# Hybrid linear-attention and window-attention block: longer planned distances, fewer places for small steps, two moved loads

## The chip, the cores and the metric

The kernel runs on one core of one Trainium2 chip. The metric is the device time of one execution in microseconds, the median of several runs. The engines are TensorE (PE, with its weight loads PEld), VectorE (DVE), ScalarE (ACT), GpSimd (POOL) and SyncE (SP), which issues nearly all DMAs.

## The reference, cut to what matters

The input is 2048 tokens of 1024 values in float32. Branch A is a gated delta rule with four heads of 128 (in the kernel in blocks of 128 tokens). Branch B is attention over a window of 128 tokens with eight query heads, two key heads and a sink logit per head.

```python
h = x @ w_in                          # q, k, v, z, b, a of A; q, k, v, z of B; two gates
dq, dk, dv = split(silu(causal_short_conv(h[:, :1536], conv_w)))
# branch A, per head, state S (128 x 128):
#   S <- exp(g_t) S;  S <- S + k_t (beta_t (v_t - S^T k_t))^T;  o_t = S^T q_t
#   evaluated in blocks with the inverse of (1 + lower triangle of beta k k^T decay)
y_a = rmsnorm(o_a) * dn_norm_w * silu(z_a)
# branch B
p   = softmax(q k^T / 8 in the band, with the sink in the denominator)
y_b = (p v) * silu(z_b)
merged = sigmoid(gate_a) * (y_a @ w_branch[0]) + sigmoid(gate_b) * (y_b @ w_branch[1])
r = ALPHA * x + merged @ w_out
y = (r - mean(r)) * rsqrt(var(r) + eps) * ln_g + ln_b
```

## The kernel before, in words

The 2048 tokens are worked in four chunks of 512. Every dense product is made from three matmuls, because each operand is split into a high and a low part: L184 (high by high), L185 and L186 (high by low), all into the PSUM tiles `mm`. The weights are split once, in the first chunk, and kept in DRAM (`kw_...`); in chunks two to four SP loads them back into `wb`, which has four buffers (L160; L158 for the last output weights). A load waits on SP's queue until its buffer is free, and what stands behind it on the queue waits too.

A chunk is a list of pieces: the string `ORDER` (kv, k0, q0, ... are projections, `g` a gate, `p` a part of the output projection of the chunk before, `w0` and `w1` the queries of branch B, `z` the gates of branch A's output), then eight `branch_b`, the first pieces of the next chunk, and eight `branch_a`. After `p` number 3 the norm of the chunk before starts (`layer_norm`).

Between dense matmuls stand small steps, which are chains over several engines. Of branch A: `front` (K^T L382, R L395, KK L406, q^T L426, KQ L432), an inverse on DVE (L947, L948) that goes through DRAM (`scrm`, `scrp`), `levels` (lv1 to lv4: L470, L477, L486, L491), and `back`. `back` is one chain through the four blocks: kS (L517, reads the state S) -> bt (DVE, L519) -> NEW (L522, L525) -> wc (DVE, L524) -> UPD (L528, L530) -> S (DVE, L529) -> the next block's kS. Of branch B: qT (L584, after the rope on DVE, L893 to L899) and per block ATT (scores, L610, L611) -> softmax (DVE L618 to L628, ACT L623 to L630) -> pT (two lots of four transposes, L637, each copied by ACT, L639) -> psY (L645) -> DVE and ACT write `yBh`, `yBl` (L650 to L653). These two tiles are in the same buffers as the rows that `layer_norm` works on, and attention starts when the norm is done. The norm is 32 times one L727 and one L728 on DVE; its table (gain and bias) comes in four quarters, `s<-in_lnp`, by SP.

PE's order is fixed in the program by the class `Order`, a planner with a clock of its own, `now`. Every dense piece advances `now` by a planned cost and then calls `run()`, which puts in every small step whose time has come. After a step its task is due again a fixed distance later: LAT_B within front and levels, LAT_S within back, LAT_SM from ATT to pT, LAT_D before lv1, LAT_Q from rope to qT, and so on. These distances are plan numbers; on the chip a step that comes too early waits. Where the program needs a task finished (`finish`), the planner jumps its clock without dense work, so that the task's steps stand one behind the other. The orders on DVE, ACT, POOL and SP follow from the same program, and each engine works its queue in order.

Of the kernel before, what the change touches and what calls it, by code (L numbers as in the profile page):

```python
# [16 lines left out]
P = 128  # L17
D = 1024
# [20 lines left out]

LAT_INV, LAT_B, LAT_S, LAT_N, LAT_SM, LAT_D, LAT_M, LAT_K, LAT_Q, LAT_Y, LAT_F, LAT_W = 29600, 2700, 2300, 7700, 9200, 11000, 9000, 1400, 7900, 11500, 4100, 2300  # L40
FIRST = ("h01", "h00", "h02")


ORDER_FIRST = "start g kv w0 g k1 g g q1 g g g z0 v1 g z1 k2 q2 v2 w1 k3 g q3 g v3 g g g g z2 z3 g g"
ORDER = "kv k0 q0 v0 k1 p p p p q1 g w0 v1 z0 k2 q2 v2 g g g k3 z1 g q3 g w1 v3 g g g g z2 g g g z3 g g g"

# [17 lines left out]
def build(tc, xt, xn, wk, wg, par, lnp, cst, out, seq=2048):  # L64
    nc = tc.nc
    NCH = seq // T
    with ExitStack() as ctx:
# [169 lines left out]
        def start(c):  # L237
# [25 lines left out]
            st.spawn("front0", front(c, 0), LAT_F)  # L263

        def window_kv(c):

            ww, more = [], ([w.rearrange("p (k c) -> p k c", k=2) for w in split(("kv", i), wk[i // 2, :, 528 * (i % 2):528 * (i % 2) + 528], 528)]
                            for i in range(4))
            ba = sm.tile([P, NB, 8], F32, name="ba")
            c.vs = [c.prev.vs[4] if c.i else None]  # L270
            for b0 in (0, 2):
                pss = [mm.tile([P, T], F32, name="mm")[:, :264] for _ in range(2)]
                yield from prod_tc(pss, (b0, b0 + 1), c.xh, c.xl, ww if b0 else kept(more, ww), lambda k: load_x(c, k))
                for b, ps in zip((b0, b0 + 1), pss):
# [9 lines left out]
            st.spawn("decay", decays(c, ba), LAT_Y)  # L284

# [13 lines left out]
        def decays(c, ba):  # L299
            c.beta, c.g = gates_small(nc, sm, ba, nea, prm[:, P_DTB:P_DTB + 4])  # L300
            flat = lambda a: a.rearrange("p b h -> p (b h)")
            new = lambda name: sm.tile([P, NB, NH], F32, name=name)
            c.nG, c.kd, c.neG, c.eGl = new("nG"), new("kd"), new("neG"), new("eGl")
            psg = pd.tile([P, T], F32, name="pd")
            tri = sm.tile([P, P], F32, name="wc", bufs=1)
            nc.vector.tensor_scalar(tri, dmask, 0.0, None, ALU.is_ge)
            nc.tensor.matmul(psg[:, :16], tri, flat(c.g), start=True, stop=True)
            nc.tensor.matmul(psg[:, 16:32], ones, flat(c.g), start=True, stop=True)
            G = psg[:, :16].rearrange("p (b h) -> p b h", h=NH)
            gg = sm.tile([P, NB, 2, NH], F32R, name="ghl", bufs=1)  # L310
# [8 lines left out]
            yield 2 * 426, 2000  # L319
# [49 lines left out]
        def front(c, h):  # L369
# [21 lines left out]
            nc.vector.tensor_scalar(nci, cc, -1.0, None, ALU.mult)  # L391
            yield 4 * PE_T, LAT_B

# [8 lines left out]
            nc.vector.tensor_tensor(qd, qd, q4, ALU.mult)  # L402
            yield PE_R, LAT_B
            psKK = p4()
# [5 lines left out]
            t0 = st.now  # L410
            yield 4 * PE_F, LAT_B

# [14 lines left out]
            for b in range(NB):  # L427
                nc.scalar.activation(junk, psQ[:, b], AF.Square, accum_out=qsum[:, b:b + 1])
            yield 4 * PE_T, LAT_B
            psKQ = p4()  # L430
# [4 lines left out]
            q_ = t4("q_", 2)  # L435
            st.spawn(f"levels{h}", levels(c, h, m2, q_), max(LAT_B, t0 + LAT_INV - st.now))
            st.spawn(f"back{h}", back(c, h, k4, q_, ktl, qd, dt, cc, ksum, qsum), max(LAT_B, t0 + LAT_INV - st.now))
            yield 4 * PE_F, 0

        def inverse(h, su, xi):  # L440

            with tc.issue_after(next(i for i in reversed(nc.cur_bb.bb.instructions) if i.engine == mybir.EngineType.DVE)):
                nc.vector.memset(view(su, 33, [[66, 16]]), 0.0)
# [4 lines left out]
        def levels(c, h, m2, q_):  # L448
# [11 lines left out]
            yield 0, LAT_D  # L460
            for i in range(4):
# [9 lines left out]
            for s in range(2):  # L471
                copy[s](x_[hi[s], :, :32], ps[s][hi[s], :, :32])
            yield 8 * PE_Q, LAT_B
            ps = [p4(), pp.tile([P, NB, P], F32, name="pp")]
# [13 lines left out]
            yield 4 * PE_T, LAT_B  # L488
# [4 lines left out]
            yield 4 * PE_T, LAT_B  # L493

        def back(c, h, k4, q_, ktl, qd, dt, cc, ksum, qsum):
# [16 lines left out]
            st.done.add(f"vdone{h}")  # L512
            yield 4 * PE_T, LAT_B
            psO = p4()
            for b in range(NB):
# [9 lines left out]
                nc.tensor.matmul(psO[:, b], qd[:, b], S[:, h], start=True, stop=False)  # L525
                yield 2 * PE_F, LAT_S
# [4 lines left out]
                yield 2 * PE_F, LAT_S  # L531

# [28 lines left out]
        def window_q(c, gp):  # L561
# [6 lines left out]
            for b0 in (0, 2):  # L568
# [25 lines left out]
        def attend(c, gp):  # L594
# [8 lines left out]
            for b in range(NB):  # L603
# [108 lines left out]
        def layer_norm(c):  # L712
            fs = []
            for b in range(NB):
# [118 lines left out]
class Order:  # L833
# [190 lines left out]
```

## Time and profile before

| what | value |
|---|---|
| time, median of 3 runs | 1668.41 us (1666.62 to 1669.23) |
| the profiled execution's own time | 1672.24 us |
| its span | 1670.40 us |
| PE busy | 1618.9 us, 97% of the span |
| PE's share of the chain that ended last | 82% |
| DVE, ACT, POOL busy | 969.3, 596.2, 92.9 us |
| mean granted TensorE clock | 0.986 of full |

The profiled execution has 1.84 us outside its span and took 3.83 us more than the median. PE is busy nearly all the time, and its matmuls are pipelined, so that a busy PE is read by the distance of the starts. A wait of PE is in brackets in the timeline, with the instruction that released it. A granted clock of 1.00 in a stretch is the 2.4 GHz level, 0.50 the 1.2 GHz level.

### The profile page before, as it was taken

How to read it: one execution, taken by the hardware profiler on the slowest of the kernel's cores; microseconds unless marked ns; L12 is line 12 of the kernel's file. 1: busy time of each engine (PE TensorE's matmuls, PEld its weight loads, DVE VectorE, ACT ScalarE, POOL GpSimd, SP SyncE). 2: the span in 40 equal slices, each digit the busy share in tenths (PEclk: the TensorE clock that was granted, in tenths of full speed). 3: DMA queues.
4: the chain of work that ended last, by engine and by line, in shares of the span. 5: the costliest groups of instructions: out<-in, count | busy, mean ns of one | idle time of the engine just before them, and what ended most of it. 6: DMA issues, size and time to landing. Idle time of an engine off the chain costs nothing.

```text
span 1670.4 us, 26939 instructions
## 1 busy us (share of the span) xinstructions
PE 1618.9 (97%) x9846; PEld 1368.2 (82%) x9846; DVE 969.3 (58%) x3005; ACT 596.2 (36%) x1688; POOL 92.9 (6%) x142
## 2 busy tenths in 40 slices
PE   8999999999998999999999999999999999999998
PEld 6877878787987878788898878888889887878788
DVE  5777687459566656323747774623482866462145
ACT  3565455424213533441301452433230254233110
POOL 2100000000000001000000000000000100000000
PEclk9999999999999999999999999999999999999999
DMA  8876575776867446457666644646666654555862
GB/s 310 260 232 222 184 245 190 244 235 216 273 207 213 135 130 168 142 163 237 191 213 205 199 128 145 172 137 190 202 190 210 221 162 119 166 162 145 284 214 83
DMA packets 189157, 323.37 MB, mean 194 GB/s; under 512 B 31072, under 2 KB 45408, under 8 KB 188896
## 3 DMA queue, kind: packets, MB, share of 16 engines
q1 hardware_dynamic: 185184, 316.40, 60.6%
q0 software_dynamic: 3840, 5.25, 1.5%
q8 instruction: 78, 1.28, 0.3%
q14 instruction: 55, 0.45, 0.1%
HBM read 244.97 MB, written 71.37 MB: 189 GB/s over the span
## 4 chain that ended last, share of the span: by engine, by line
PE 82%; DVE 7%; DMA 7%; ACT 2%; issue 1%; SPq 1%; POOL 0%; DVEq 0%; ACTq 0%; POOLq 0%
PE mm L184 22%; PE mm L186 22%; PE mm L185 22%; PE pp L645 2%; PE pp L637 2%; DMA s<-in_lnp 2%; DMA w<-in_xt 1%; PE pp L610 1%; PE pp L611 1%; PE pd L432 1%; DVE wb L165 1%; PE pd L517 1%; PE pd L528 1%; DMA xl<-kw_o 1%; PE pd L406 1%
## 5 line engine op out<-in xcount | busy, mean ns | idle before, releaser
L184 PE MATMUL mm<-xh,wb 128*128 128x512 f32 x1128 | 468.6, 415 | 0.0
L186 PE MATMUL mm<-xh,wb 128*128 128x512 f32 x1128 | 448.0, 397 | 0.0
L185 PE MATMUL mm<-xl,wb 128*128 128x512 f32 x1128 | 446.8, 396 | 0.0
L186 PEld LDWEIGHTS mm<-xh,wb 128*128 128x128 f32 x1128 | 213.7, 189 | 50.3
L184 PEld LDWEIGHTS mm<-xh,wb 128*128 128x128 f32 x1128 | 214.5, 190 | 45.6 <-issue 6.5
L185 PEld LDWEIGHTS mm<-xl,wb 128*128 128x128 f32 x1128 | 215.2, 191 | 38.8
L184 PE MATMUL mm<-wb,xh 128*128 128x256 f32 (+1 forms) x384 | 113.5, 296 | 1.8 <-DVE kr L899 0.9
L184 PE MATMUL mm<-wb,s 128*128 128x256 f32 x384 | 110.4, 287 | 0.0
L185 PE MATMUL mm<-wb,xh 128*128 128x256 f32 (+1 forms) x384 | 108.9, 284 | 0.0
L186 PE MATMUL mm<-wb,xl 128*128 128x256 f32 (+1 forms) x384 | 108.7, 283 | 0.0
L185 PE MATMUL mm<-wb,s 128*128 128x256 f32 x384 | 108.4, 282 | 0.0
L186 PE MATMUL mm<-wb,s 128*128 128x256 f32 x384 | 108.4, 282 | 0.0
L165 DVE TENSOR_TENSOR wb<-w,wb 128x512 fp32r<-128x512 f32 (+1 forms) x110 | 75.4, 686 | 46.3 <-ACT wb L164 45.5
L164 ACT ACTIVATE wb<-w 128x512 fp32r<-128x512 f32 (+1 forms) x110 | 69.1, 629 | 84.4 <-PE mm L186 58.1
L623 ACT ACTIVATE s<-s,nm 128x256 f32<-128x256 f32 (+1 forms) x128 | 62.5, 490 | 57.1 <-DVE nm L620 56.6
L947 DVE TENSOR_TENSOR xt<-su,xi 128x16 f32<-128x16 f32 (+15 forms) x256 | 76.3, 298 | 5.3
L948 DVE TENSOR_REDUCE xi<-xt 128x8 f32<-128x16 f32 (+15 forms) x256 | 74.6, 291 | 4.9
L184 PEld LDWEIGHTS mm<-wb,xh 128*128 128x128 f32 x384 | 72.9, 190 | 2.7 <-issue 2.5
L184 PEld LDWEIGHTS mm<-wb,s 128*128 128x128 f32 x384 | 73.1, 190 | 0.8
L185 PEld LDWEIGHTS mm<-wb,xh 128*128 128x128 f32 x384 | 72.9, 190 | 0.5
L185 PEld LDWEIGHTS mm<-wb,s 128*128 128x128 f32 x384 | 73.0, 190 | 0.1
L186 PEld LDWEIGHTS mm<-wb,s 128*128 128x128 f32 x384 | 73.0, 190 | 0.0
(660 smaller groups left out, 2997.4 us busy)
## 6 DMA issues: line engine op xcount, KB each, us to landing
wb<-kw_h SPq DMA_DIRECT2D x96, 512.0 KB, 4.1
wb<-kw_g SPq DMA_DIRECT2D x96, 512.0 KB, 4.0
w<-in_wg SPq DMA_DIRECT2D x106, 256.0 KB, 4.2
wb<-kw_b SPq DMA_DIRECT2D x48, 512.0 KB, 4.4
wb<-kw_o SPq DMA_DIRECT2D x36, 512.0 KB, 4.1
kw_h<-wb SPq DMA_DIRECT2D x32, 512.0 KB, 3.9
kw_g<-wb SPq DMA_DIRECT2D x32, 512.0 KB, 3.7
wb<-kw_q SPq DMA_DIRECT2D x24, 512.0 KB, 3.9
```

Of the source, the lines that this page charges most:

```text
L164: nc.scalar.activation(hi, raw, AF.Copy)
L165: nc.vector.tensor_tensor(lo, raw, hi.bitcast(F32), ALU.subtract)
L184: nc.tensor.matmul(ps, sh, mh, start=(first and i == 0), stop=False, skip_group_check=shared)
L185: nc.tensor.matmul(ps, sh, ml, start=False, stop=False, skip_group_check=shared)
L186: nc.tensor.matmul(ps, sl, mh, start=False, stop=(last and i == n), skip_group_check=shared)
L406: nc.tensor.matmul(psKK[:, b], k4[:, b], k4[:, b], start=True, stop=True)
L432: nc.tensor.matmul(psKQ[:, b], k4[:, b], q4[:, b], start=True, stop=True)
L623: nc.scalar.activation(ss[v][:, g, k0:], ss[v][:, g, k0:], AF.Exp, bias=nm[:, v, g:g + 1], scale=0.125, accum_out=su[:, v, g:g + 1])
L637: nc.tensor.transpose(psp[:, kb, g], ss[v][:, g, P * kb:P * kb + P], ident)
L645: nc.tensor.matmul(psY[64 * v:64 * v + 64], c.vs[b + kb][:, 64 * v:64 * v + 64], pTs[v][:, kb], start=(kb == kbs[0]), stop=(kb == 1))
L947: nc.vector.tensor_tensor(tx[:, :, :, :n], u, x, ALU.mult)
L948: nc.vector.tensor_reduce(xi[:, :, i:i + 2], tx[:, :, :, :n], AX.X, ALU.add)
```

## The change

In chunks two to four the distances within front, levels and back are 600 ns longer, ATT to pT 2300, before lv1 2000, rope to qT 2600, and the step in `decays` 1500. In `ORDER` the piece `w1` stands one gate earlier. Each quarter of the norm's table is asked for one quarter ahead, and the norm's planned distances are longer. Each half of the last output weights is issued behind the last SP instruction placed so far. Last, `run()` is called only when 1900 ns of the planner's clock have gone by since the last time.

```diff
+LAT_B, LAT_S, LAT_SM, LAT_D, LAT_Q, LAT_Y, LAT_G = (2700, 3300), (2300, 2900), (9200, 11500), (11000, 13000), (7900, 10500), (11500, 11500), (2000, 3500)
-ORDER = "kv k0 q0 v0 k1 p p p p q1 g w0 v1 z0 k2 q2 v2 g g g k3 z1 g q3 g w1 v3 g g g g z2 g g g z3 g g g"
+ORDER = "kv k0 q0 v0 k1 p p p p q1 g w0 v1 z0 k2 q2 v2 g g g k3 z1 g q3 w1 g v3 g g g g z2 g g g z3 g g g"
+        latest = lambda engine: next(i for i in reversed(nc.cur_bb.bb.instructions) if i.engine == engine)
...
-                yield PE_F, LAT_S
+                yield PE_F, LAT_S[c.i > 0]
...
-                yield 8 * PE_T, LAT_SM
+                yield 8 * PE_T, LAT_SM[c.i > 0]
...
+            def load_lg(eg):
+                lgs.append(pa.tile([P, 2, 256], F32, name="s"))
+                nc.sync.dma_start(out=lgs[eg], in_=bass.AP(tensor=lnp.tensor, offset=lnp.offset + 256 * eg, ap=[[0, P], [D, 2], [1, 256]]))
+            load_lg(0)
...
-                yield None, 2500
+                yield None, 2600
...
-                lg = pa.tile([P, 2, 256], F32, name="s")
-                nc.sync.dma_start(out=lg, in_=bass.AP(tensor=lnp.tensor, offset=lnp.offset + 256 * eg, ap=[[0, P], [D, 2], [1, 256]]))
+                if eg < 3:
+                    load_lg(eg + 1)
+                lg = lgs[eg]
...
-                    yield None, 1800
+                    yield None, 2200
...
+            st.quantum = 1900.0 if i else 0.0
...
                 if i == NCH - 1 and d in (1, 4):
-                    last_weights(c, d // 3)
+                    with tc.issue_after(latest(mybir.EngineType.SP)):
+                        last_weights(c, d // 3)
...
                 self.now += dur
-                self.run()
+                if self.now >= self.next:
+                    self.run()
+                    self.next = self.now + self.quantum
```

Every engine has the same instructions as before, in another order; the first chunk's are unchanged. On PE, the runs of small steps without a dense matmul between them go from 287 to 211 in chunks two to four, so 76 of them are joined to a neighbour. Lines of the changed kernel are 2 to 16 higher: L614 and L615 are ATT, L521 kS, L526 and L529 NEW, L532 and L534 UPD, L641 pT, L649 psY, L186 to L188 dense.

Such groups without a dense matmul inside are: in w0, at the start of its gates, q^T, UPD, KQ, kS, NEW, qT, UPD (third and fourth chunk; the same steps in another order in the second); at v2 of the second chunk psY, lv2, ATT, K^T, lv3, R, lv4, KK, vT; in each chunk, directly before the first `branch_b`, NEW, UPD, both lots of pT and psY, which before stood among the last gates.

PE at the piece k3 of the third chunk, before: between the scores and the weights' transposes of a block, and between the two lots of transposes, stand dense matmuls.

```order
L184 MATMUL mm<-xh,wb 128x512
L185 MATMUL mm<-xl,wb 128x512
L186 MATMUL mm<-xh,wb 128x512
L517 MATMUL pd<-S,k 128x128
L522 MATMUL pd<-bt,q__9801 128x128
L525 MATMUL pd<-S,qd 128x128
L528 MATMUL pd<-wc,ktl 128x128
L530 MATMUL pd<-wc,dt 128x128
L637 MATMUL pp<-ct,s 128x128 x4
L184 MATMUL mm<-xh,wb 128x512
L185 MATMUL mm<-xl,wb 128x512
L186 MATMUL mm<-xh,wb 128x512
```

The same place after, from the last scores on:

```order
L615 MATMUL pp<-kTl_145,qT_9586 128x256
L526 MATMUL pd<-bt,q__9799 128x128
L529 MATMUL pd<-S,qd 128x128
L532 MATMUL pd<-wc,ktl 128x128
L534 MATMUL pd<-wc,dt 128x128
L521 MATMUL pd<-S,k 128x128
L641 MATMUL pp<-ct,s 128x128 x4
L526 MATMUL pd<-bt,q__9799 128x128
L529 MATMUL pd<-S,qd 128x128
L641 MATMUL pp<-ct,s 128x128 x4
L532 MATMUL pd<-wc,ktl 128x128
L534 MATMUL pd<-wc,dt 128x128
```

What moved: the six dense matmuls behind the scores, and the six between the two lots of transposes, are gone from here; two blocks of `back` and both lots stand in one group, with psY behind them. The same is at k3 of the other two chunks (in the second with lv1, lv2 and lv3 in it).

SP in the third chunk, before (`kw_q0` are the weights of w0, `kw_zb` of its gates):

```order
L160 DMA wb_9777<-kw_q01_1_668 128x2x512
L160 DMA wb_9909<-kw_zb0_0_814 128x2x512
L725 DMA s_9802<-in_lnp 128x2x256
L725 DMA s_9853<-in_lnp 128x2x256
L417 DMA scrm1_149<-m2_9698 32x4x32 x4
L160 DMA wb_9935<-kw_zb0_1_844 128x2x512
```

And after:

```order
L162 DMA wb_9721<-kw_q01_1_668 128x2x512
L162 DMA wb_9856<-kw_zb0_0_814 128x2x512
L162 DMA wb_9877<-kw_zb0_1_844 128x2x512
L721 DMA s_9705<-in_lnp 128x2x256
L721 DMA s_9804<-in_lnp 128x2x256
L421 DMA scrm1_149<-m2_9700 32x4x32 x4
```

What moved: the third and fourth quarter of the norm's table stand behind one more weight load.

DVE at the same place, before, from the m of the inverse to the state (L727 and L728 are the norm, L524 wc, L529 S):

```order
L409 SCALAR_TENSOR_TENSOR m_9698<-pd,nci,dt 128x128 x4
L524 TENSOR_SCALAR wc<-pd,cc 128x128
L727 SCALAR_TENSOR_TENSOR yBh<-yBh,mv,s 128x256 x2
L727 SCALAR_TENSOR_TENSOR yBl<-yBl,mv,s 128x256 x2
L727 SCALAR_TENSOR_TENSOR yBh<-yBh,mv,s 128x256 x2
L727 SCALAR_TENSOR_TENSOR yBl<-yBl,mv,s 128x256
L728 SCALAR_TENSOR_TENSOR yBh<-yBh,rs,s 128x256
L727 SCALAR_TENSOR_TENSOR yBl<-yBl,mv,s 128x256
L728 SCALAR_TENSOR_TENSOR yBh<-yBh,rs,s 128x256
L728 SCALAR_TENSOR_TENSOR yBl<-yBl,rs,s 128x256 x2
L728 SCALAR_TENSOR_TENSOR yBh<-yBh,rs,s 128x256
L529 SCALAR_TENSOR_TENSOR S<-S,eGl,pd 128x128
```

And after, from the norm's third quarter to the state (L738 and L739 are the norm, L528 wc, L533 S, L913 rope):

```order
L738 SCALAR_TENSOR_TENSOR yBh<-yBh,mv,s 128x256 x2
L738 SCALAR_TENSOR_TENSOR yBl<-yBl,mv,s 128x256 x2
L739 SCALAR_TENSOR_TENSOR yBh<-yBh,rs,s 128x256
L738 SCALAR_TENSOR_TENSOR yBh<-yBh,mv,s 128x256 x2
L738 SCALAR_TENSOR_TENSOR yBl<-yBl,mv,s 128x256 x2
L739 SCALAR_TENSOR_TENSOR yBh<-yBh,rs,s 128x256
L528 TENSOR_SCALAR wc<-pd,cc 128x128
L739 SCALAR_TENSOR_TENSOR yBl<-yBl,rs,s 128x256 x2
L739 SCALAR_TENSOR_TENSOR yBh<-yBh,rs,s 128x256 x2
L913 TENSOR_TENSOR rope<-mm,ct 128x64 x2
L739 SCALAR_TENSOR_TENSOR yBl<-yBl,rs,s 128x256 x2
L533 SCALAR_TENSOR_TENSOR S<-S,eGl,pd 128x128
```

What moved: wc, which stood ahead of the norm's last two quarters, stands behind 10 of their 16 instructions, and S behind all 16.

## Rows read from the trace of the kernel before

**Rows 1.** The page's busy times of the engines.
```profile
PE 1618.9 (97%) x9846; PEld 1368.2 (82%) x9846; DVE 969.3 (58%) x3005; ACT 596.2 (36%) x1688; POOL 92.9 (6%) x142
```

**Rows 2.** Waits of PE, 381 us to the end: us in total, times, longest.
```profile
PE pp L637 <- ACT s L630: 6.4, 3, 2.1
PE pd L517 <- DVE S L529: 5.0, 4, 2.5
PE pp L584 <- DVE rsq L884: 3.4, 1, 3.4
PE mm L184 <- DMA wb<-kw_b: 2.6, 2, 1.6
PE pd L395 <- DVE ktl L385: 2.4, 3, 1.2
...
PE pd L470 <- DMA p__4808<-scrp: 1.9, 1, 1.9
```

**Rows 3.** Stretches: length, busy time of each engine, granted clock, DMA share, GB/s.
```profile
440.31:443.73 3.42, 3.42 (x28) 3.36 (x23) 1.48 (x5) 0.27 (x1) 0.00 (x0) 0.50 0.96 302
...
508.58:515.41 6.83, 5.87 (x16) 4.46 (x17) 6.52 (x38) 2.33 (x5) 1.08 (x2) 0.50 0.98 360
...
901.00:916.00 15.00, 12.67 (x105) 12.42 (x106) 13.55 (x45) 3.42 (x12) 1.01 (x1) 1.00 0.61 189
1000.10:1003.51 3.41, 3.34 (x10) 2.58 (x10) 2.90 (x12) 1.69 (x6) 1.01 (x1) 0.50 0.00 0
```

**Rows 4.** PE timeline, last branches: start, length, instruction, wait before it.
```profile
1582.56 0.47 PE L184 MATMUL mm<-yBh,wb 128*128 128x512 f32 x1 [1.64 <-DMA wb<-kw_b]
```

**Rows 5.** DVE timeline, third chunk, piece w0.
```profile
907.48 0.34 DVE L524 TENSOR_SCALAR wc<-pd,cc 128x128 f32<-128x128 f32 x1
909.27 0.88 DVE L727 SCALAR_TENSOR_TENSOR yBh<-yBh,mv,s 128x256 f32<-128x256 f32 x2 [1.45 <-DMA s<-in_lnp]
...
914.43 0.34 DVE L529 SCALAR_TENSOR_TENSOR S<-S,eGl,pd 128x128 f32<-128x128 f32 x1
```

**Rows 6.** SP timeline, the same place.
```profile
905.55 0.89 SPq L725 DMA_DIRECT2D s<-in_lnp  x2
...
909.45 0.52 SPq L160 DMA_DIRECT2D wb<-kw_zb  x1
```

**Rows 7.** PE timeline, the same place: the first matmul of w0.
```profile
898.99 0.36 PE L184 MATMUL mm<-wb,xh 128*128 128x256 f32 x1
```

**Rows 8.** PE timeline, third chunk, piece k3.
```profile
992.82 0.36 PE L610 MATMUL pp<-kT,qT 128*128 128x256 f32 x1
...
996.08 0.49 PE L522 MATMUL pd<-bt,q__9801 128*128 128x128 f32 x2 [0.45 <-DVE bt L519]
...
997.01 0.49 PE L528 MATMUL pd<-wc,ktl 128*128 128x128 f32 x2 [0.22 <-DVE wc L524]
...
999.86 1.30 PE L637 MATMUL pp<-ct,s 128*128 128x128 f32 x4 [2.14 <-ACT s L630]
```

**Rows 9.** ACT timeline, the same place.
```profile
999.31 1.69 ACT L630 ACTIVATE s<-s,sum 128x256 f32<-128x256 f32 x4
...
1001.20 0.60 ACT L639 ACTIVATE pT<-pp 128x512 f32<-128x512 f32 x1
```

**Rows 10.** PE timeline: NEW among dense matmuls, then NEW joined to pT.
```profile
1042.07 0.39 PE L522 MATMUL pd<-bt,q__10559 128*128 128x128 f32 x2
...
1042.44 0.37 PE L184 MATMUL mm<-wb,xh 128*128 128x256 f32 x1
1042.64 0.28 PE L185 MATMUL mm<-wb,xh 128*128 128x256 f32 x1
1042.76 0.28 PE L186 MATMUL mm<-wb,xl 128*128 128x256 f32 x1
...
1124.26 0.38 PE L522 MATMUL pd<-bt,q__11204 128*128 128x128 f32 x2
...
1124.70 0.60 PE L637 MATMUL pp<-ct,s 128*128 128x128 f32 x4
```

More of the change, by code (lines that the diff above doesn't have):

```diff
@@ L38 @@
 PE_R, PE_F, PE_T, PE_Q = 216, 218, 109, 45
-LAT_INV, LAT_B, LAT_S, LAT_N, LAT_SM, LAT_D, LAT_M, LAT_K, LAT_Q, LAT_Y, LAT_F, LAT_W = 29600, 2700, 2300, 7700, 9200, 11000, 9000, 1400, 7900, 11500, 4100, 2300
+LAT_INV, LAT_N, LAT_M, LAT_K, LAT_F, LAT_W = 29600, 7700, 9000, 1400, 4100, 2300
+LAT_B, LAT_S, LAT_SM, LAT_D, LAT_Q, LAT_Y, LAT_G = (2700, 3300), (2300, 2900), (9200, 11500), (11000, 13000), (7900, 10500), (11500, 11500), (2000, 3500)
 FIRST = ("h01", "h00", "h02")
 ORDER_FIRST = "start g kv w0 g k1 g g q1 g g g z0 v1 g z1 k2 q2 v2 w1 k3 g q3 g v3 g g g g z2 z3 g g"
-ORDER = "kv k0 q0 v0 k1 p p p p q1 g w0 v1 z0 k2 q2 v2 g g g k3 z1 g q3 g w1 v3 g g g g z2 g g g z3 g g g"
+ORDER = "kv k0 q0 v0 k1 p p p p q1 g w0 v1 z0 k2 q2 v2 g g g k3 z1 g q3 w1 g v3 g g g g z2 g g g z3 g g g"
 EARLY = (("kv", "window1"), ("k0", "back2"), ("q0", "qdone3"))
@@ L283, in window_kv @@
                     st.spawn(f"kT{b}", key_rows(c, b, kr), LAT_K)
-            st.spawn("decay", decays(c, ba), LAT_Y)
+            st.spawn("decay", decays(c, ba), LAT_Y[c.i > 0])
         def key_rows(c, b, kr):
@@ L318, in decays @@
             nc.scalar.activation(flat(c.eGl), psg[:, 16:32], AF.Exp)
-            yield 2 * 426, 2000
+            yield 2 * 426, LAT_G[c.i > 0]
             psr = pd.tile([P, T], F32, name="pd")
@@ L391, in front @@
             nc.vector.tensor_scalar(nci, cc, -1.0, None, ALU.mult)
-            yield 4 * PE_T, LAT_B
+            yield 4 * PE_T, LAT_B[c.i > 0]
             psR = p4()
@@ L402, in front @@
             nc.vector.tensor_tensor(qd, qd, q4, ALU.mult)
-            yield PE_R, LAT_B
+            yield PE_R, LAT_B[c.i > 0]
             psKK = p4()
@@ L410, in front @@
             t0 = st.now
-            yield 4 * PE_F, LAT_B
+            yield 4 * PE_F, LAT_B[c.i > 0]
             sm_ = scr_m[h % 2]
@@ L428, in front @@
                 nc.scalar.activation(junk, psQ[:, b], AF.Square, accum_out=qsum[:, b:b + 1])
-            yield 4 * PE_T, LAT_B
+            yield 4 * PE_T, LAT_B[c.i > 0]
             psKQ = p4()
@@ L435, in front @@
             q_ = t4("q_", 2)
-            st.spawn(f"levels{h}", levels(c, h, m2, q_), max(LAT_B, t0 + LAT_INV - st.now))
-            st.spawn(f"back{h}", back(c, h, k4, q_, ktl, qd, dt, cc, ksum, qsum), max(LAT_B, t0 + LAT_INV - st.now))
+            st.spawn(f"levels{h}", levels(c, h, m2, q_), max(LAT_B[c.i > 0], t0 + LAT_INV - st.now))
+            st.spawn(f"back{h}", back(c, h, k4, q_, ktl, qd, dt, cc, ksum, qsum), max(LAT_B[c.i > 0], t0 + LAT_INV - st.now))
             yield 4 * PE_F, 0
         def inverse(h, su, xi):
-            with tc.issue_after(next(i for i in reversed(nc.cur_bb.bb.instructions) if i.engine == mybir.EngineType.DVE)):
+            with tc.issue_after(latest(mybir.EngineType.DVE)):
                 nc.vector.memset(view(su, 33, [[66, 16]]), 0.0)
@@ L459, in levels @@
                                   in_=at(scr_p[h % 2], 1024 * i, [[32, 32], [4096, NB], [1, 32]]))
-            yield 0, LAT_D
+            yield 0, LAT_D[c.i > 0]
             for i in range(4):
@@ L472, in levels @@
                 copy[s](x_[hi[s], :, :32], ps[s][hi[s], :, :32])
-            yield 8 * PE_Q, LAT_B
+            yield 8 * PE_Q, LAT_B[c.i > 0]
             ps = [p4(), pp.tile([P, NB, P], F32, name="pp")]
@@ L482, in levels @@
                 copy[1 - s](q_[lo[s], :, hi[s]], ps[s][lo[s], :, :32])
-            yield 12 * PE_Q, LAT_B
+            yield 12 * PE_Q, LAT_B[c.i > 0]
             ps = p4()
@@ L487, in levels @@
             copy[0](x_[64:], ps[64:, :, :64])
-            yield 4 * PE_T, LAT_B
+            yield 4 * PE_T, LAT_B[c.i > 0]
             ps = p4()
@@ L492, in levels @@
             copy[1](q_[:64, :, 64:], ps[:64, :, :64])
-            yield 4 * PE_T, LAT_B
+            yield 4 * PE_T, LAT_B[c.i > 0]
         def back(c, h, k4, q_, ktl, qd, dt, cc, ksum, qsum):
@@ L512, in back @@
             st.done.add(f"vdone{h}")
-            yield 4 * PE_T, LAT_B
+            yield 4 * PE_T, LAT_B[c.i > 0]
             psO = p4()
@@ L525, in back @@
                 nc.tensor.matmul(psO[:, b], qd[:, b], S[:, h], start=True, stop=False)
-                yield 2 * PE_F, LAT_S
+                yield 2 * PE_F, LAT_S[c.i > 0]
                 ps = pd.tile([P, T], F32, name="pd")[:, :P]
@@ L530, in back @@
                 nc.tensor.matmul(psO[:, b], dt[:, b], wc, start=False, stop=True)
-                yield 2 * PE_F, LAT_S
+                yield 2 * PE_F, LAT_S[c.i > 0]
             osum = sm.tile([P, NB], F32, name="osum")
@@ L573, in window_q @@
                     rope(nc, sm, qr[b], pss[b0 // 2][:, b], 4, cos[:, c.i * NB + b0 + b], sin[:, c.i * NB + b0 + b])
-                st.spawn(f"qT{b0}", query_rows(c, b0, qr), LAT_Q)
+                st.spawn(f"qT{b0}", query_rows(c, b0, qr), LAT_Q[c.i > 0])
             for g in range(2):
@@ L838, in __init__ @@
     def __init__(self):
-        self.now, self.tasks, self.done = 0.0, [], set()
+        self.now, self.tasks, self.done, self.next, self.quantum = 0.0, [], set(), 0.0, 0.0
     def spawn(self, name, task, after):
```

2 lines of the change are left out of this document (1 added, 1 removed).

## The prediction

> **What bounds the kernel now.** I read the engines' busy times first: PE is busy for 1618.9 of 1670.4 us [rows 1], and no other engine comes near. All engines keep their instructions, so no work goes away on PE; what can change is how long PE stands still and how long its clock is low. The waits of PE come second. Over chunks two to four the view's 13 rows add up to 29.0 us, of which the six shown make 21.7 [rows 2]. Third come stretches of time with the granted clock. Behind several of these waits PE runs at 0.50, the 1.2 GHz level, for 3.41 or 6.83 us [rows 3]. PE is full of dense work there, so half of such a stretch is lost, 1.7 us for the short one. There are seven such stretches in chunks two to four, of which three are shown; in units of 3.41 us they are eight (the one of 6.83 counts as two), 13.6 us in all. Not every wait has one: from 901 to 916 us, with over 2 us of PE not busy, the clock is 1.00 [rows 3]. So the reachable loss is about 43 us, 2.6%, and the change shifts parts of it.
>
> All sums are made against the profiled execution, 1672.24 us; for the forecast I take 3.83 us off, the distance to the median.
>
> **The change part by part.**
>
> *Last output weights.* PE waits twice for `wb<-kw_b`, 2.6 us in all [rows 2], the longer time 1.64 [rows 4], because loads of the output weights stand between those of the branch weights on SP. With each half in one block behind the branch weights issued so far, the branch weight that PE needs next is ahead. Saved: 2.6, and 0.3 for the first matmul behind each wait, which comes late too: **-2.9**. What is late next is the output weight itself, needed only by the last projection. The bounds are -2.9 and 0.
>
> *lv1 of the second chunk.* The wait of 1.9 for `p_<-scrp` [rows 2] has a half-clock stretch behind it (440.31 to 443.73) [rows 3]. LAT_D is 2.0 us longer, as long as the wait: -1.9, and -1.7 for the clock: **-3.6**. Bounds: -3.6, and 0 if the inverse itself comes later by as much, being on a DVE that has other work.
>
> *The piece w0 (place A).* Here the norm is on DVE while `back` needs DVE for wc and S. In the third chunk wc runs at 907.48, ahead of the norm's last two quarters, which start at 909.27 after 1.45 of waiting for the table; S runs at 914.43 in the midst of them [rows 5], and PE waits for it at kS. Over the three chunks this place holds the waits of qT for the rope (3.4), of R (2.4) and nearly all of kS's for S (5.0) [rows 2], 10.8 us. To these I add 3.5 for its shorter waits and for the late first matmul behind each: 14.3 before.
>
> After, the table's last two quarters are asked for early in the program, but on SP they stand one weight load later. Before, they were issued at 905.55 and that load at 909.45 [rows 6]; in between it stood behind `scrm`, which waits for DVE, so that I place it some 0.5 us behind 905.55 now. The norm's last half then starts 0.5 us later, at 909.7, and wc stands behind 10 of its instructions. Two take 0.80 us (the row's 0.88 less the overlap with the next) [rows 5]: wc is ready at 909.7 + 4.0 + 0.3 = 914.0, 6.5 us later than before, and S behind all 16, at 916.5, 2 us later. From there kS (0.2), DVE's queue ahead of bt (rope, dt's product, a step of the inverse: 1.5), bt and wc (0.35 each [rows 5]), NEW and UPD (0.45 each [rows 10]) and the handovers (0.6) take 3.9 us, to 920.4. PE has only that group to do meanwhile; its work of the piece, without waits, is 16.9 us from the first matmul at 898.99 [rows 7], to 915.9. It stands still for about 4.6 us. Three times 4.6 is 13.8: **-0.5**. The bounds are wide: -8 if the early request makes the norm end before `back` needs DVE, +5 if S comes 1.7 us later still. The clock I leave as it is, with three units before in this place (two of them the row of 6.83) and three after.
>
> *The piece k3 (place C).* The scores start at 992.82, and pT of the same block starts 7.04 us later, at 999.86, with three waits on the way, 0.45, 0.22 and 2.14 [rows 8]; with 0.2 for each late first matmul it cost 3.5 us, and the same three stand in each chunk. What PE waits for is the softmax, whose last ACT instructions begin at 999.31 [rows 9]. Nothing shortens that chain. But the six dense matmuls behind the scores, 6 x 0.23 us, are gone from there, as the order shows. The small steps that are left are ATT (1.0), NEW and UPD (0.45 each [rows 10]) and one kS (half of such a step, 0.2): 2.1 us. So PE stands still for 7.04 - 2.1 = 4.9. psY stands a few small steps behind the second pT and needs ACT's copy, 0.60 [rows 9]: 0.6 more. That is 5.5, or 2.0 more than before, in each of three chunks: **+6.0**. Bounds: 0, if the softmax comes as much earlier on DVE and ACT as PE has less to do, and twice the sum, +12.
>
> *A new group in the second chunk (place B, piece v2)*: psY, lv2, ATT, K^T, lv3, R, lv4, KK, vT with no dense work between. The trace of before does not show it. Nearest are PE's waits for a result that DVE gives right behind the matmul, 0.22 and 0.45 [rows 8]; four such steps at 0.45 make **+1.8**, with bounds of 0 and 4.
>
> *The end of the attention (place E).* Before the first `branch_b` of each chunk now stand NEW, UPD, both lots of pT and psY in one group. UPD waits 0.22 for wc [rows 8]; psY waits for two copies of 0.60 each [rows 9], less what PE does meanwhile: 1.0. Three times 1.25 is **+3.75**. Bounds: 0 and 8, the upper one if the first `branch_b` waits for the last `yBh` as well.
>
> *The clock.* C, E and B stand still longer or newly. Behind C's 2.14 there was one half-clock stretch [rows 3]. I add half a unit (0.85) for each of the three C and one B, since waits here do and don't bring one: **+3.4**, with bounds of -3 and +8.
>
> *Joined groups, one dense gate's place for w1, the longer LAT_B.* I cost these at 0. NEW among dense matmuls takes from 1042.07 to 1042.64, less one normal spacing of 0.12 (1042.64 to 1042.76): 0.45 us. Joined to pT it takes from 1124.26 to 1124.70: 0.44 [rows 10]. So a step costs the same alone and joined, and 76 joins bring 0.8 us at most.
>
> The Trainium skill would have it otherwise ("TensorE: Matmul & The Clock Gate", "Step-by-step: what each phase is for"): the drain of a matmul is hidden under the next one's fill, and one that stands alone pays it. By the page's constant for the full clock (398 cycles at 2.4 GHz, 0.166 us) an estimate of 76 saved drains would be 12.6 us. The row with NEW speaks against it, 0.45 against 0.44.
>
> Sum: -2.9 - 3.6 - 0.5 + 6.0 + 1.8 + 3.75 + 3.4 = +7.95, say +8: 1680 for the profiled execution, and 1668.41 + 8 = **1676.4 us** for the median.
>
> **The rivals.**
>
> *Faster: the longer distances take the waits away.* That speaks for it that R, kS and lv1 wait because they come early in the plan. Then the weights and lv1 bring -6.5, A goes from 14.3 to 7 (-7.3), and C, E and B cost no more than before: 1668.4 - 13.8 = 1654.6, and with half of it 1661. Whether the norm's last half is done before PE comes to the group in w0 decides it. Against it: wc now stands behind the norm in DVE's queue.
>
> *No change.* The weights and lv1 (-6.5) pay for B and E (+5.55), and C costs nothing, because its softmax is not slowed by dense work: -1 with A, 1667.5. For it: DVE does the inverse among the softmax and may have less of it there. Against it: PE's wait at C comes from a chain on DVE and ACT that is the same length wherever it starts.
>
> *Slower by more: the clock.* Ten groups without dense work (A, C, E in three chunks, B once). If each brings one half-clock unit more than I counted, that is 10 x 1.7 - 3.4 = +13.6 on top of +8: 1690. The stretch after each group decides: waits of 1.9 and 2.1 us had half clock behind them, but the third chunk's w0, with over 2 us of waits in parts, had none [rows 2, 3].
>
> *Joins are worth a drain each.* Two lone steps that become one group would save at most 0.166 each if the seam were free; then +8 - 12.6 gives 1663.8. The measured 0.01 per join speaks against it.
>
> **How the numbers follow.** The forecast has 0.46, the faster case 0.15, no change 0.16, the clock 0.18, the joins 0.05. The forecast's own range is 1670 to 1682: half of each bound (A and C 3, the clock 3, B and E 2.3), added by squares, which is 6. The range that leaves out 2 in 10 has at its low end half of the faster case, and at its high end nearly all of the clock case: 1662 to 1690. What a measurement can tell from no change is 0.2%, so the limits are 1665.1 and 1671.7. Faster by more: all of the faster case, the joins, and 0.03 of no change: 0.23. Within: 0.13 of no change and 0.04 of the forecast: 0.17. Slower: 0.60.
>
> **What would show it.** Right: at the last branches no wait for `kw_b`; lv1 of the second chunk without a wait; in each chunk waits of 4 to 5 us in all at k3, for the softmax, with half clock behind it; in w0 a wait for wc of some 4 us; PE's waits in chunks two to four at 33 to 38 us in place of 29. Wrong: k3's wait under 3 us, or w0's waits gone, or, with the same waits, a number of half-clock units far from ten, or steps in a joined group that follow each other faster than 0.44 us per NEW.

## The result, and the profile after

The changed kernel takes 1717.01 us (median of 4 runs, 1715.21 to 1720.86) against 1668.82 before (the three runs of the table above and one more): ratio 1.0285, 95% interval 1.0267 to 1.0303. Slower was right; 8 us were forecast and 48 came. The profiled execution has a span of 1715.9 us, 45.5 more.

PE is still the engine that bounds. Of the 45.5 us its busy time [rows 1] takes 15.7, mostly since the same matmuls last longer at half clock, and its idle time the other 29.8.

```profile
PE 1634.6 (95%) x9846; PEld 1380.3 (80%) x9846; DVE 976.0 (57%) x3005; ACT 596.3 (35%) x1688; POOL 96.1 (6%) x142
```

PE's waits from 381 us to the end (total, times, longest), as in [rows 2]:

```profile
PE pd L532 <- DVE wc L528: 12.2, 9, 2.9
PE pp L649 <- ACT pT L643: 6.5, 5, 2.8
PE pp L641 <- ACT s L634: 6.1, 4, 2.1
PE pd L430 <- DVE m L413: 5.1, 4, 1.8
...
PE pd L521 <- DVE S L533: 3.1, 5, 1.3
PE pd L474 <- DMA p__10731<-scrp: 2.9, 1, 2.9
PE pd L474 <- DMA p__14851<-scrp: 2.8, 1, 2.8
...
PE mm L186 <- DMA wb<-kw_b: 2.6, 2, 1.5
...
PE mm L186 <- DVE yBh L705: 1.8, 1, 1.8
```

The 21 rows of the view add up to 55.3 us, 26.3 more than before. The waits for wc have grown most, psY's for ACT's copies and q^T's for the inverse's m (L413) are new, and lv1, which waited in the second chunk, waits in the third and fourth.

Four of the stretches at half clock, with the columns of [rows 3]: in w0 of the second chunk (13.65 us), in w0 of the third, at lv1 of the third, and at the end of the attention.

```profile
500.09:513.74 13.65, 8.34 (x30) 7.40 (x31) 10.15 (x44) 3.86 (x14) 0.88 (x2) 0.50 0.70 235
...
926.76:933.59 6.83, 4.68 (x19) 3.99 (x18) 6.40 (x31) 1.48 (x4) 0.00 (x0) 0.50 1.00 371
...
1032.57:1039.40 6.83, 6.22 (x29) 4.89 (x30) 2.11 (x6) 1.10 (x3) 0.00 (x0) 0.50 0.17 40
1189.58:1192.99 3.41, 3.41 (x11) 2.08 (x8) 1.80 (x8) 1.70 (x5) 1.01 (x1) 0.50 0.33 125
```

In units of 3.41 us there are 19 such in chunks two to four, against 8. The sums of these stretches, before and after:

```profile
sum 27.31, PE 26.26 PEld 21.78 DVE 21.89 ACT 10.39 POOL 4.84; mean PE 3.75 PEld 3.11 DVE 3.13 ACT 1.48 POOL 0.69
```

```profile
sum 64.85, PE 52.91 PEld 42.70 DVE 40.01 ACT 24.84 POOL 4.54; mean PE 4.81 PEld 3.88 DVE 3.64 ACT 2.26 POOL 0.41
```

By the prediction's 1.7 us a unit, eleven more would be 18.8 us. But half a unit is lost only where PE is busy throughout, and in the 37.5 us added it was busy for 26.65; the rest are waits, which are counted already. The clock is then worth some 13.3 us (an estimate, half of the 26.65). With the waits' 26.3 that is 39.6 of the 45.5 us. There are 49 waits in place of 33; the prediction's 0.2 us for the late first matmul behind each makes 3.2 more, an estimate too, and the last 2.7 us are not assigned. They are a loss, so nothing here points to a gain from the 76 joined groups.

**w0, third chunk.** DVE's timeline, to be read beside [rows 5]: the norm's last half starts when its table lands; wc comes 4.0 us later and S 6.9.

```profile
921.09 0.88 DVE L738 SCALAR_TENSOR_TENSOR yBh<-yBh,mv,s 128x256 f32<-128x256 f32 x2 [1.67 <-DMA s<-in_lnp]
...
925.05 0.34 DVE L528 TENSOR_SCALAR wc<-pd,cc 128x128 f32<-128x128 f32 x1
...
927.95 0.34 DVE L533 SCALAR_TENSOR_TENSOR S<-S,eGl,pd 128x128 f32<-128x128 f32 x1
```

PE's rows with waits at that place (UPD, kS, NEW), 4.2 us in all:

```profile
925.45 0.49 PE L532 MATMUL pd<-wc,ktl 128*128 128x128 f32 x2 [2.02 <-DVE wc L528]
928.34 0.79 PE L521 MATMUL pd<-S,k 128*128 128x128 f32 x2 [1.13 <-DVE S L533]
930.15 0.79 PE L526 MATMUL pd<-bt,q__8886 128*128 128x128 f32 x2 [1.02 <-DVE bt L523]
```

The last two last 0.79 in place of 0.46 to 0.49: the clock has already fallen.

**k3, third chunk**, to be read beside [rows 8]: UPD waits 1.29 for wc and pT 2.14 for the softmax; with a kS between them (0.22) 3.65 us, where it was 2.81. It is UPD's wait that has grown, from 0.22; pT's is the same.

```profile
1014.42 0.49 PE L532 MATMUL pd<-wc,ktl 128*128 128x128 f32 x2 [1.29 <-DVE wc L528]
...
1017.98 0.94 PE L641 MATMUL pp<-ct,s 128*128 128x128 f32 x4 [2.14 <-ACT s L634]
```

**lv1 of the third head, third chunk.** It waits 2.95 us, and in the fourth chunk 2.80. Part of the cause stands 25 us earlier on DVE: the load of `su` for the inverse was issued at 998.4 and took 5.3 us, to 1003.7, but the inverse's first instruction (L447) runs at 1008.33, because S (L533) stands ahead of it in DVE's queue and waits for PE's UPD.

```profile
1008.02 0.35 DVE L533 SCALAR_TENSOR_TENSOR S<-S,eGl,pd 128x128 f32<-128x128 f32 x1 [2.33 <-PE pd L532]
1008.33 0.07 DVE L447 MEMSET su<- 128x16 f32 x1
```

That is only part, since the kernel before had such a hold too (2.6 us in the fourth chunk). The rest shows from m to lv1, before and then after:

```profile
973.40 1.12 DVE L409 SCALAR_TENSOR_TENSOR m<-pd,nci,dt 128x128 f32<-128x128 f32 x4
1005.79 1.73 SPq L458 DMA_DIRECT2D p__10777<-scrp  x4
1016.37 0.21 PE L470 MATMUL pd<-p__10777,m 32*32 32x32 f32 x1
```

```profile
992.49 1.12 DVE L413 SCALAR_TENSOR_TENSOR m<-pd,nci,dt 128x128 f32<-128x128 f32 x4
1030.18 1.73 SPq L462 DMA_DIRECT2D p__10731<-scrp  x4
1032.95 0.31 PE L474 MATMUL pd<-p__10731,m 32*32 32x32 f32 x2 [2.95 <-DMA p__10731<-scrp]
```

From m to the load of `p_` it is 37.7 us in place of 32.4, of which the first instruction's delay is 2.5. And PE, without its wait, is ready for lv1 37.5 us behind m in place of 43.0. So the inverse came later by about as much as lv1 came earlier, although LAT_D had been made longer.

**The end of the attention, second chunk.** psY waits 2.81 and 0.36 us for the copies of pT (PE's rows). On ACT the copies (L643) stand behind conversions of the next chunk's input (L234), which wait for their DMA. The fourth chunk, which has no next chunk to convert, has 0.53 there.

```profile
764.24 0.65 PE L649 MATMUL pp<-pT,vb 128*64 128x256 f32 x2 [2.81 <-ACT pT L643]
765.24 1.08 PE L649 MATMUL pp<-pT,vb 128*64 128x256 f32 x6 [0.36 <-ACT pT L643]
```

```profile
761.37 0.63 ACT L234 ACTIVATE xh<-w 128x512 fp32r<-128x512 f32 x1 [1.56 <-DMA w<-in_xt]
...
762.81 0.63 ACT L234 ACTIVATE xh<-w 128x512 fp32r<-128x512 f32 x1 [0.56 <-DMA w<-in_xt]
...
763.60 0.59 ACT L643 ACTIVATE pT<-pp 128x512 f32<-128x512 f32 x1
```

**The last weights.** The wait of [rows 4] has moved from `branch_b` to `branch_a`, where the second eight loads now stand between branch weights; it is 2.6 us as before.

```profile
1641.54 0.47 PE L186 MATMUL mm<-yAh,wb 128*128 128x512 f32 x1 [1.16 <-DMA wb<-kw_b]
...
1651.62 0.47 PE L186 MATMUL mm<-yAh,wb 128*128 128x512 f32 x1 [1.49 <-DMA wb<-kw_b]
```

### The profile page after: what moved, and what is told of

Read it like the earlier page. It is cut to its first block, busy times and chain, and to the rows that moved or that the text cites. A ratio compares the mean times of both kernels' runs of the same rounds, so it can differ in the third digit from the quotient of the medians.

```text
span 1715.9 us, 26934 instructions
## 1 busy us (share of the span) xinstructions
PE 1634.6 (95%) x9846; PEld 1380.3 (80%) x9846; DVE 976.0 (57%) x3005; ACT 596.3 (35%) x1688; POOL 96.1 (6%) x142
## 4 chain that ended last, share of the span: by engine, by line
PE 79%; DVE 9%; DMA 7%; ACT 3%; issue 2%; SPq 1%; POOL 0%; DVEq 0%; ACTq 0%; POOLq 0%
PE mm L186 22%; PE mm L187 21%; PE mm L188 21%; PE pp L649 2%; DMA s<-in_lnp 1%; PE pp L641 1%; DMA w<-in_xt 1%; PE pd L532 1%; PE pp L614 1%; DVE wb L167 1%; PE pd L436 1%; PE pd L521 1%; PE pd L526 1%; PE pd L534 1%; PE pp L615 1%
## 5 line engine op out<-in xcount | busy, mean ns | idle before, releaser
L186 PE MATMUL mm<-xh,wb 128*128 128x512 f32 x1128 | 467.4, 414 | 0.0
L188 PE MATMUL mm<-xh,wb 128*128 128x512 f32 x1128 | 448.3, 397 | 0.0
L188 PEld LDWEIGHTS mm<-xh,wb 128*128 128x128 f32 x1128 | 214.0, 190 | 50.9
L186 PEld LDWEIGHTS mm<-xh,wb 128*128 128x128 f32 x1128 | 215.1, 191 | 46.9 <-issue 5.0
L186 PE MATMUL mm<-wb,xh 128*128 128x256 f32 (+1 forms) x384 | 111.3, 290 | 1.6 <-DVE kr L915 0.9
L186 PE MATMUL mm<-wb,s 128*128 128x256 f32 x384 | 109.6, 285 | 1.8 <-DVE yBh L705 1.8
L188 PE MATMUL mm<-wb,s 128*128 128x256 f32 x384 | 108.5, 283 | 0.0
L188 PE MATMUL mm<-wb,xl 128*128 128x256 f32 (+1 forms) x384 | 108.2, 282 | 0.0
L186 PEld LDWEIGHTS mm<-wb,s 128*128 128x128 f32 x384 | 73.1, 190 | 2.6 <-DVE yBh L705 2.0
L186 PEld LDWEIGHTS mm<-wb,xh 128*128 128x128 f32 x384 | 72.4, 189 | 2.5 <-issue 2.0
L188 PEld LDWEIGHTS mm<-wb,s 128*128 128x128 f32 x384 | 73.1, 190 | 0.0
L188 PEld LDWEIGHTS mm<-wb,xl 128*128 128x128 f32 x384 | 72.4, 189 | 0.0
```

What stands on the lines that cost most here:

```text
L186: nc.tensor.matmul(ps, sh, mh, start=(first and i == 0), stop=False, skip_group_check=shared)
L188: nc.tensor.matmul(ps, sl, mh, start=False, stop=(last and i == n), skip_group_check=shared)
```

## The experiments

Each ratio is to the kernel before, with its 95% interval. Waits are PE's from 381 us on, units are half-clock stretches counted as above. The planner's own figures (forced jumps, groups, lateness) come from the program.

**Taking the change apart: e1, e2, e3.**

```diff
-            st.quantum = 1900.0 if i else 0.0     # e1 and e3
+            st.quantum = 0.0
-LAT_B, LAT_S, LAT_SM, LAT_D, LAT_Q, LAT_Y, LAT_G = (2700, 3300), (2300, 2900), (9200, 11500), ...
+LAT_B, LAT_S, LAT_SM, LAT_D, LAT_Q, LAT_Y, LAT_G = (2700, 2700), (2300, 2300), (9200, 9200), ...   # e2 and e3
```

Dots in a list, here and below, stand for its other distances; e2 and e3 have the old ones throughout.

> The changed kernel with run() called after every dense cost again (quantum 0); longer distances, order, norm and weights stay. Theory D (the longer distances make the loss: where the program forces a task to its end the planner's clock jumps further, and what is due by that clock, lv1 above all, comes after less real work): still slow, 1700 to 1715 us, lv1 of head 2 waits 5 us or more in chunks three and four (its work distance from KK falls to 28 us). Theory Q (fewer places make the loss, since a step that is let in late stands in a chain without dense work): back to 1668 to 1680 us, few waits at k3 and w0.

> The changed kernel with the old distances; the quantum of 1900 ns, order, norm and weights stay. Theory D: 1670 to 1685 us, no wait at lv1 of head 2 in chunks three and four beyond 1 us. Theory Q: 1700 to 1715 us, with waits at w0 and k3 as in the changed kernel.

> The changed kernel with the old distances and without the quantum, so only the norm's table, w1's place and the last weights are changed. Both theories: 1663 to 1673 us, since these three move few waits; theory N, a third one (the norm and its table hold DVE or SP at w0 and make the loss): over 1680 us with waits for wc and S at w0 of 4 us and more.

| kernel | ratio | waits, units |
|---|---|---|
| before | 1 | 29.0, 8 |
| e3, neither | 0.9988 (0.9975 to 1.0000) | 29.3, 5 |
| e1, longer distances, no quantum | 1.0087 (1.0068 to 1.0106) | 35.7, 8 |
| e2, quantum, old distances | 1.0174 (1.0155 to 1.0193) | 45.9, 15 |
| changed, both | 1.0285 (1.0267 to 1.0303) | 55.3, 19 |

Norm, order and last weights together cost nothing, so theory N falls. Both others cost, 1.0% (16 us) and 1.9% (30 us by the medians), and they add up. D and Q are each half right, and neither met a range: e1 came out at 1684.6 us, under D's range and over Q's, and had no wait at lv1 of that head; e2 at 1698.6, over D's and under Q's.

**The inverse planned later: e4.**

```diff
-LAT_INV = 29600
+LAT_INVS = (29600, 37000)   # the second value in chunks two to four, for levels and for back
...
```

> The changed kernel with the planned distance from KK to lv1 at 37.0 us in place of 29.6 in chunks two to four, so that 37 us of PE work lie between KK and lv1 of head 2 in chunks three and four in place of 31. Theory D: lv1's waits there (2.9 and 2.8 us and the half clock behind them) go, 8 to 13 us faster than the changed kernel, 1704 to 1709 us. Rival: the inverse's DVE steps are themselves late behind PE's steps, so the later lv1 only pushes back's steps into the forced stretches: 1714 us or more.

1700.75 us, 1.0178 (1.0147 to 1.0209): 16 us faster than the changed kernel, more than expected. PE's waits at lv1 for its DMA are a seventh of what they were:

```profile
PE pd L474 <- DMA p__14880<-scrp: 0.4, 1, 0.4
PE pd L474 <- DMA p__10760<-scrp: 0.4, 1, 0.4
```

Waits fall to 44.5 us and units to 13, and the four units at these two lv1 are gone. So lv1 with its clock is a large single piece of the loss. It isn't all of the 16 us: the edit starts `back` later as well, and of the 10.8 us of waits that went, 4.9 are these two.

**Size of the quantum, and distances shortened by half of it: e5, e6, e10.**

```diff
-            st.quantum = 1900.0 if i else 0.0     # e5, on e2
+            st.quantum = 950.0 if i else 0.0
-LAT_B, LAT_S, LAT_SM, ... = (2700, 2700), (2300, 2300), (9200, 9200), ...     # e6, on e2
+LAT_B, LAT_S, LAT_SM, ... = (2700, 1750), (2300, 1350), (9200, 8250), ...
-LAT_B, LAT_S, LAT_SM, ... = (2700, 3300), (2300, 2900), (9200, 11500), ...    # e10, on the changed kernel
+LAT_B, LAT_S, LAT_SM, ... = (2700, 2350), (2300, 1950), (9200, 10550), ...
```

> The kernel with neither (old distances; norm's table, w1's place and last weights changed), and a quantum of 950 ns in place of 0. It joins few groups: 272 against 274 without a quantum and 234 with 1900 ns in chunks two to four. Theory L (lateness: a step comes on average half a quantum late, so that chains run into the places where the program forces them): 1668 to 1675 us, since the planner's forced jumps stay at 63 us. Theory J (joined groups cost): 1667 to 1672 us. A loss in proportion to the quantum, by any other cause, would give 1680 to 1686.

> Quantum 1900 ns as in the run with old distances, but LAT_B, LAT_S, LAT_SM, LAT_D, LAT_Q and LAT_G 950 ns shorter than the old ones in chunks two to four, so that a step is on average no later than without a quantum. Groups stay joined (239 against 234), the planner's forced jumps fall from 76 to 48 us. Theory L: 1665 to 1678 us, most of the 30 us come back. Theory J (what costs is that steps of different chains stand in a row, so that one step's wait holds the others): 1690 us or more.

> The changed kernel, quantum 1900 ns and all, with its six distances each 950 ns shorter (3300 to 2350, 2900 to 1950, 11500 to 10550, 13000 to 12050, 10500 to 9550, 3500 to 2550). Groups stay joined (220 against 207 in the changed kernel), forced jumps fall from 136 to 67 us, as in the kernel before. Theory L: 1665 to 1676 us, although all that the change added is there. If the distances add by themselves what they added without a quantum: 1684.

e5 0.9987 (0.9971 to 1.0004), which tells nothing apart, since it joins hardly any group; e6 0.9986 (0.9971 to 1.0001), waits 30.1, units 4; e10 1.0040 (1.0022 to 1.0059), 1678 us, 2 us above its range. With the same quantum and nearly as few groups, shorter distances bring back all of the 30 us in e6 and 39 of 48 in e10. e6 against e3 also prices the join: 239 groups in place of 274, and the same time (0.9986 and 0.9988). Joining by itself costs and gains nothing; joining chains that are late costs.

**Which distances: e7, e8, e9.**

```diff
+LAT_B, LAT_S = (2700, 3300), (2300, 2900)                            # e7, on e3
+LAT_SM, LAT_D, LAT_Q, LAT_G = (9200, 11500), (11000, 13000), (7900, 10500), (2000, 3500)   # e8, on e3
+LAT_B, LAT_S, LAT_SM, ... = (2700, 3650), (2300, 3250), (9200, 10150), ...  # e9, on e3: all six 950 longer
```

> The kernel with neither, and of the distances only LAT_B and LAT_S longer (3300 and 2900). Forced jumps of the planner's clock go from 63 to 82 us and lv1 of head 2 has 31.2 us of work behind KK in place of 37.2. Theory D (forced jumps and what falls due too early by them): 1678 to 1686 us, the larger part of the 16 us that all distances cost. Rival (long waits are what is too long): under 1672.

> The kernel with neither, and LAT_SM, LAT_D, LAT_Q and LAT_G longer, LAT_B and LAT_S old. Forced jumps go from 63 to 71 us, and lv1 keeps 36 to 39 us. Theory D: 1666 to 1674 us; the softmax's wait at k3 is shorter only if it isn't forced there. Rival: 1678 or more.

> The kernel with neither, no quantum, and LAT_B, LAT_S, LAT_SM, LAT_D, LAT_Q and LAT_G 950 ns longer than the old ones in chunks two to four: the mean lateness that a quantum of 1900 ns gives, without its joining (265 groups against 274; the quantum made 234). The planner's forced jumps go from 63 to 110 us. Theory L (lateness): 1685 to 1705 us. Theory J (joining): under 1675.

e7 0.9996 (0.9981 to 1.0012), which theory D had at 1678 or more: a miss. e8 0.9978 (0.9959 to 0.9998). e9 1.0087 (1.0057 to 1.0117), 1686.7 us. Each kind of distance costs nothing alone, both together 16 us (e1): the loss isn't in proportion to the distances. Nor are the planner's forced jumps its measure: 82 us of them in e7 cost nothing, 76 in e2 30 us. Where the loss begins was not found.

**What the quantum adds: e12, e13, e14.** It cost 30 us where 950 ns of lateness without joining cost 17, though in the planner a step of `back` came on average 1.00 us late with it and 0.52 without.

```diff
-LAT_SM = (9200, 9200)                             # e12, on e2
+LAT_SM = (9200, 6300)
+        only = lambda t: dve is None or dve == t[1].startswith(("inverse", "norm"))
...
                     self.next = self.now + self.quantum
+                else:
+                    self.run(True)    # e13, on e2; e14: self.run(False)
```

> Quantum 1900 ns with the old distances, as in the run that cost 30 us, but ATT to pT at 6300 in place of 9200 ns in chunks two to four. In the planner a step of the attention comes on average 1.46 us after it is due with this quantum and 0.73 without; a block has four such steps, so 2900 ns takes back what the quantum adds to a block. Groups: 225 in place of 234. Theory LA (what the quantum costs beyond the lateness of the other chains is the attention's lateness, which pushes its end into branch_b and w1): 1675 to 1688 us, no wait for yBh at the first branch_b. Rival J (joined groups themselves): 1693 us or more.

> Quantum 1900 ns with the old distances, but the tasks that have only DVE instructions and their DMAs (the inverse and the norm) are let in after every dense cost, as without a quantum. PE's order is the same as in the run with old distances, which cost 30 us. Theory V (the quantum's part beyond lateness comes from DVE's queue: the inverse's steps are put in later, behind steps of other chains that wait for PE, and hold them up in turn): 1675 to 1688 us. Rival J (PE's order itself, joined groups met by results that are late): 1694 to 1704 us.

> The converse: only the inverse and the norm wait for the quantum, all steps with PE are let in after every dense cost (285 groups against 274 with neither). Theory V: 1678 to 1690 us, the inverse late at lv1. Rival J: 1666 to 1674 us.

e12 1.0181 (1.0155 to 1.0208), 1701.9 us: the wait for yBh at `branch_b` went, as expected, but lv1 waited 4.4 to 4.6 us in each chunk in its place; theory LA fell. e13, with e2's order on PE, but the inverse and the norm let in on DVE as without a quantum: 1.0148 (1.0120 to 1.0176), 1697.8 us, so most of the loss stays. PE's first waits in e2, and then in e13, are nearly the same:

```profile
PE pp L641 <- ACT s L634: 9.6, 4, 4.0
PE pd L526 <- DVE bt L523: 8.4, 4, 4.3
```

```profile
PE pp L641 <- ACT s L634: 9.4, 4, 3.2
PE pd L526 <- DVE bt L523: 7.8, 4, 4.2
```

e14, the quantum for the inverse and the norm alone: 0.9930 (0.9913 to 0.9947), 1659.2 us, waits 23.9, 2 units. Theory V expected a loss there; J expected none, and it was a gain. So the quantum's cost is in the order of the steps with PE in them, not in the places of the inverse and the norm. DVE's and ACT's parts of those steps moved with PE's, and no run parts the two. Why e14 gains was not taken apart; it has 5.4 us fewer waits and three units fewer than e3.

**Versions that beat both: e11, e15, e16.**

```diff
-                if i == NCH - 1 and d in (1, 4):
+                if i == NCH - 1 and d % 2 == 0:      # a quarter of the sixteen loads each
...
# e11 on e8; e15 on e14; e16 on e14 with e8's distances
```

> The run with only the long distances longer, and the last output weights' sixteen loads spread over four places (two of each kind of tile before branch_a 0, 2, 4 and 6) in place of eight at once before 1 and 4. The two waits for kw_b at the end, 1.1 and 1.0 us there, should go: 2 us faster than that run, 1661 to 1667 us. Rival: the loads are late for the last projection instead, and the time stays.

> The run in which only the inverse and the norm wait for the quantum, with the last output weights' loads spread over four places. The two waits for kw_b at the end, 1.1 and 1.1 us there, should go: 1656 to 1659 us. If the spreading did nothing of its own: 1659 to 1661.

> The same with LAT_SM, LAT_D, LAT_Q and LAT_G longer too. If the two gains add (4 us from the long distances' side): 1653 to 1657 us. Rival: the long distances and the inverse's new places meet as the distances did with each other, and it is slower than the run without them: 1660 to 1670.

e11 0.9950 (0.9932 to 0.9968), e15 **0.9919 (0.9897 to 0.9941)**, 1656.8 us, e16 0.9956 (0.9941 to 0.9971). The waits for `kw_b` are gone in e11 and e15. What that gave in time isn't clear of the noise: e15's interval overlaps with e14's, and e11's with e8's. In e16 the gains don't add.

## Why the prediction was wrong

The direction held, and so did the kind of account: the time is PE's waits and the half-clock stretches with them, and a join by itself is worth nothing. The Trainium skill's rule of a drain saved at each join ("TensorE: Matmul & The Clock Gate", "Step-by-step: what each phase is for") finds no support: by the estimate of 0.166 us each, the 35 joins of e6 over e3 would have gained 5.8 us, and the time stayed.

Two things failed, the waits by some 20 us and the clock by some 12. Forecast for the waits was about +6.5 us, and as a sign 33 to 38 in all; measured 55.3. Read from PE's timelines by place, in us (the single waits add up to 26.5, the rounded rows of the view to 26.3):

| term | forecast | waits measured |
|---|---|---|
| last weights | -2.6 | 0 |
| lv1, with the dense matmul behind it | -1.9 | +6.0 |
| A, w0 | -0.5 | +4.3 |
| C, k3 | +6.0 | +2.2 |
| B, v2 | +1.8 | +2.0 |
| E, end of the attention | +3.75 | +7.2 |
| all other places | 0 | +4.8 |

The first step that failed is **"Joined groups, ... the longer LAT_B. I cost these at 0."** The seam is free, as e6 shows, but the order it makes is not: the quantum with the old distances costs 30 us, and most of that stays when the inverse and the norm are let in as before (e13). I priced a few places by their waits and held the rest for unchanged, where K^T waits 1.0 in the third and the fourth chunk, and q^T and KQ at w1 1.5 together in every chunk.

Second, **lv1** was a gain of 3.6 "of the second chunk" only. There its wait went, but the next dense matmul waited 1.8 for the norm (`yBh`) instead, with half clock behind it, so nothing was gained; in the third and fourth chunk a wait of 3 us came up each. The bound had named a later inverse, but for the second chunk alone. I had looked at the plan's longer distance before lv1, while lv1 came 5.5 us earlier behind m and the inverse 5.3 later. e4, which starts `back` later too, gains 16 us.

Third is **the clock**: "I add half a unit (0.85) for each of the three C and one B", 3.4 us, and -1.7 at lv1. Measured were 11 more units, some 13 us. That such groups bring more was a rival of its own, and its 1690 was the upper end; it took one unit a group, while w0 of the second chunk has four where it had two, and w0 of the third, which had none before, two. A unit also cost less than the 1.7 of the sum, about 1.2, since PE stood still in part of it. That 18.8 and the 26.3 of the waits come to 45.1, so near to 45.5, is luck.

Of the single places: **A** was right in mechanism and size in the third chunk (wc 4.0 us behind the table, a wait of 4.2 for 4.6), and 5.2 in the fourth, but too small in the second (7.5). There 1.8 and 2.7 are waits for m and S behind the norm; the last 2.9 is for a wc that the norm, done at 503.9, did not hold:

```profile
508.34 0.33 DVE L528 TENSOR_SCALAR wc<-pd,cc 128x128 f32<-128x128 f32 x1 [2.39 <-issue]
508.72 0.80 PE L532 MATMUL pd<-wc,ktl 128*128 128x128 f32 x2 [2.91 <-DVE wc L528]
```

What held DVE for these 2.39 us the profile doesn't name; the inverse's load landed just before, at 508.3. **B** was right, 2.0 for 1.8, in one wait of KK and not in four. **C** was too large: 0.84 more in the third and fourth chunk and 0.6 in the second, in place of 2.0, since pT's wait stayed at 2.14 (1.47 in the second) while other waits took up the time. **E** was too small: 3.4 and 3.0 us in the second and third chunk, 0.75 in the fourth, for 1.25; the copy was held by ACT's queue, which the sum left out. **The last weights** failed: -2.9 was forecast, 0 came, since the wait moved to `branch_a`; spread over four places (e11) it goes. In the rival of no change, -6.5 + 5.55 and A's -0.5 make -1.45, not -1; nothing hangs on it.

What stays open is why late chains and joined groups together cost more than either. The places of the inverse and the norm on DVE aren't it (e13), nor the attention's distance alone (e12); which groups on PE carry it was not taken apart.

## What to carry to other kernels

A planned distance that is too long is not free: with both kinds longer the kernel lost 16 us, and under the quantum shorter distances brought back 30 and 39. That a longer chain is forced to its end, and that other steps then fall due early by the planner's clock, fits lv1, but as the measure of the loss it isn't shown (e7). Price a wait with the half-clock stretch around it, and count only the time that PE is busy in it; here that was three tenths of the loss. Change one kind of distance at a time: two that cost nothing apart cost 16 us together, and the part that gained (the quantum for DVE's tasks only) was hidden under the one that lost.

## What was not expected of the hardware

A wait's price in clock varied more than its length: the 4.2 us of waits in w0 of the third chunk had 6.83 us at half clock with them, the 7.5 us in the second 13.65 (PE was busy for 8.34 of them), the 3.65 at k3 3.41. In the kernel before, over 2 us of waits in that same place had none [rows 3].
